# Hybrid decoder step: larger triangular base blocks on VectorE, chains over the prompt ahead in the scheduler's order, samples spaced wider

## The chip, the cores and the metric

The kernel runs on one core of one Trainium2 chip. The metric is the device time of one execution in microseconds (us), of which three were taken. The engines of the core are called PE (TensorE, matrix products), DVE (VectorE), ACT (ScalarE), POOL (GpSimd) and SP (which here issues transfers).

## The reference

One inference step of a trunk of two layers, model width 2048, fp32, for a prompt of 256 tokens and eight samples of one token each, which share the weights. A layer adds to x, in turn, mixers, cross attention and a SwiGLU feed-forward part of width 5632. The mixers are four mLSTM heads and eight heads of gated delta net (GDN) from one input projection. The change concerns the GDN heads. For the prompt, chunk by chunk of 64 tokens:

```python
A = jnp.where(strict, decay_ts * kk * bc[:, None, :, :], 0.0)
rhs = vc - eg[..., None] * jnp.einsum('bthd,bhde->bthe', kc, S)
U = lax.linalg.triangular_solve(A, rhs, left_side=True, lower=True, unit_diagonal=True)
wu = bc[..., None] * U
o = eg[..., None] * einsum(qc, S) + einsum(qk, wu)
S_new = exp(g_end) * S + einsum(wend, kc, wu)
```

For a sample the same recurrence is one step: products of its key and query with the state S (128x128 for each head and sample), and an update of S by one outer product.

## The kernel before

All tokens stand side by side, 264 columns (256 of the prompt, 8 samples), with the model's width over the partitions. Weights come from memory in blocks of 512 KB (`raw`, four buffers). ACT rounds a block to the fast matmul type (`wh`), DVE subtracts for the remainder (`wl`); `wh` and `wl` have three buffers each. `block` does so for each block, with a scheduling priority of its own (`PRIO`). PE then makes three products for each 128x128 piece (`xh` with `wh`, `xl` with `wh`, `xh` with `wl`), 24 matmuls `acc` a block. This stream of `acc` matmuls goes through the whole kernel; the other work of the mixers stands between its matmuls.

What stands where is set in two steps. First the program's text: `stream` calls `pump` after each pair of pieces, and `pump` advances generators (`chains`) whose due time has come. The clock for this counts only PE's matmuls by their size; a generator says by `yield 13000.0` that it wants to go on that many ns of this clock later. Then a list scheduler orders the instructions on each engine; `tc.high_priority(offset)` moves instructions ahead in its choice. The compiled order is fixed: an engine takes its instructions one after another, and an instruction that waits holds up those behind it.

The GDN heads are handled in four groups of two heads. For each group of each layer three generators run: `gdn_decay` (the gates' decays `E`), `gdn_prompt` and `gdn_sample`.

`gdn_prompt` solves the triangular system by the inverse of four 128x128 matrices at once (two heads, two pairs of chunks). `N` is the strictly lower matrix, `NT` its transpose made by PE, `A` a copy of that. `base_blocks` inverts the diagonal blocks of size `BASE` on DVE: it goes over the columns from the last to the first, with `Dt<-u,Dt` (a product, written into the spare part of `Dt`) and `u<-u,Dt` (a subtraction) for each, and a 32x32-block transpose for each three columns. A last transpose and four copies by ACT (`Dm<-u`) put the blocks into `Dm`, and `Dt` is its transpose. Then `gdn_prompt` doubles the blocks: PE multiplies (`pp<-Dm,A`), DVE masks (`Pf<-pp,up`), PE multiplies again (`pd<-Pf,Dt`), DVE subtracts (`Dm<-Dm,pd`) and transposes `Dm` anew. From 8 this takes four doublings to 128; those from 8 and 16 use full 128x64 matmuls and the masks `up8` and `up16`.

`gdn_sample` gathers the samples' columns on POOL (`kv`, `kqf`), lets PE make `dks` (two transposes and 32 small products with `S`), and works on 8 rows on ACT and DVE (`dkn`, `dqn`, `dvn`, `junk` for squares), to the operands `k3` and `r3` (in the rows `k` and `r`) of the update. `rank1` masks `r3` by four samples at a time (`wm`, eight for each head, two buffers of four), PE makes the outer products `dS`, and DVE adds them to `S`, which is written out. The tiles `kv`, `kqf`, `k3` and `r3` are the same for all groups. `mlstm_sample` does likewise for the mLSTM heads.

Of the kernel before, what the change touches and what calls it, by code (L numbers as in the profile page):

```python
# [27 lines left out]
MEM = 256  # L28
EPS = 1e-6
WB, VB, SB, NV = 10, 6, 7, 6  # L30
BASE = 8
PRIO = 1000
Q0, K0, V0, O0 = 0, 512, 1024, 2048
IF0 = 3072
GQ0, GK0, GV0, GZ0 = 3080, 4104, 5128, 6152
# [13 lines left out]
def kernel(ctx: ExitStack, tc: tile.TileContext, io: dict, outs: list):  # L49
# [16 lines left out]
    clock, chains = [0.0], []  # L66
# [11 lines left out]

    def step(c):
        try:  # L80
            c[0] = next(c[1]) + clock[0]
        except StopIteration:
            chains.remove(c)

    def spawn(gen, after=0.0):
        c = [clock[0] + after, gen]
        chains.append(c)
        return c

# [452 lines left out]
    class Mix:  # L542

        def __init__(self, mx):
            self.mx = mx

        def w(self, name, shape=(4, P)):
            return self.mx.tile([P] + list(shape), F32, name=name, tag="w", bufs=WB)
# [72 lines left out]
    def gdn_prompt(l, g, s, G, M, R):  # L621
        h0 = 2 * g
        q, k, v = s
# [52 lines left out]
        for i in range(4):  # L676
            tr(pa[:, i * P:(i + 1) * P], N[:, i])
        copy(A, four(pa))
        yield 13000.0
        b = BASE  # L680
        while b < P:
            def halves(t, which, i=None):
# [104 lines left out]
    def gdn_sample(l, g, s, G, M, R, S, smp):  # L787

        h0 = 2 * g
        kv, k3, r3, kqf = smp[:4]  # L790
        for kind, at in ((1, 0), (0, 32), (2, 64)):
            pool.tensor_copy(out=kv[:, :, at:at + NB], in_=s[kind][:, :, T:C])
            if kind < 2:
                pool.tensor_copy(out=kqf[:, :, at:at + 41 * 7 + 1:41], in_=s[kind][:, :, T:C])
        yield 7500.0
        while not G.ready:
            yield 500.0
        pks = ps("dks")
        for j in range(2):
            tr(pks[:, T + j * P:T + (j + 1) * P], kv[:, j])  # L800
        for j in range(2):
            for b in range(NB):
                mm(pks[:40, j * P:(j + 1) * P], kqf[:, j, b * 40:(b + 1) * 40], S[:, j, b], b == 0, b == NB - 1)
        kn, qn, vN = M.n("dkn"), M.n("dqn"), M.n("dvn")
        for i, (d, f) in enumerate(((kn, 1.0), (qn, 1.0), (vN, 0.5))):
            copy(d, pks[32 * i:32 * i + NB, T:].rearrange("p (h t) -> p h t", h=2), scale=f)
        qk = M.c("dqk", (2, 2))[:NB]
        c = M.c("dc", (2,))[:NB]
        for j in range(2):
            act.activation(M.junk(NB)[:, :P], kn[:, j], AF.Square, accum_out=qk[:, 0, j:j + 1])  # L810
            act.activation(M.junk(NB)[:, :P], qn[:, j], AF.Square, accum_out=qk[:, 1, j:j + 1])
        dve.tensor_scalar(out=qk, in0=qk, scalar1=4.0 * EPS, scalar2=None, op0=ALU.add)
        power(qk, hm)
        tt(qn, qn, kn, ALU.mult)
        dve.tensor_reduce(out=c, in_=qn, axis=AX.X, op=ALU.add)
        rk, rq = qk[:, 0], qk[:, 1]
        egn, beta = G.gn[:, h0:h0 + 2], G.gn[:, 8 + h0:10 + h0]
        a1, er, bk = (M.c(x, (2,))[:NB] for x in ("da1", "der", "dbk"))
        stt(a1, rk, -1.0, egn, ALU.mult, ALU.mult)
        tt(bk, rk, beta, ALU.mult)  # L820
        dve.tensor_scalar(out=rq, in0=rq, scalar1=DK ** -0.5, scalar2=None, op0=ALU.mult)
        tt(er, rq, egn, ALU.mult)
        tt(c, c, rq, ALU.mult)
        tt(c, c, bk, ALU.mult)
        oN = qn
        for j in range(2):
            stt(vN[:, j], pks[:NB, j * P:(j + 1) * P], a1[:, j:j + 1], vN[:, j], ALU.mult, ALU.add)
            dve.tensor_scalar(out=oN[:, j], in0=pks[32:32 + NB, j * P:(j + 1) * P], scalar1=er[:, j:j + 1],
                              scalar2=None, op0=ALU.mult)
            stt(oN[:, j], vN[:, j], c[:, j:j + 1], oN[:, j], ALU.mult, ALU.add)  # L830
        tt(kn, kn, bc(bk, 2, P), ALU.mult)
        three(k3, kn, False)
        three(r3[:, :, :P], vN, True)
        yield 10000.0
        ev = G.gs[:, h0 * NB:(h0 + 2) * NB].rearrange("p (h b) -> p h b", h=2)
        for j in range(2):
            yield from rank1(S[:, j], k3[:, j], r3[:, j], ev[:, j], M.mx, P)
            nc.sync.dma_start(out=s_S[l, :, h0 + j].rearrange("b k v -> k b v"), in_=S[:, j])
        q = M.c("dq", (2,))[:NB]
        for j in range(2):  # L840
            act.activation(M.junk(NB)[:, :P], oN[:, j], AF.Square, accum_out=q[:, j:j + 1])
        dve.tensor_scalar(out=q, in0=q, scalar1=1.0 / DK, scalar2=EPS, op0=ALU.mult, op1=ALU.add)
        power(q, hm)
        tt(oN, oN, bc(q, 2, P), ALU.mult)
        yield 2500.0
        while R.z is None:
            yield 500.0
        pb = ps("db")
        for j in range(2):
            tr(pb[:, j * NB:(j + 1) * NB], oN[:, j], NB)  # L850
        x = M.c("dx", (2, NB))
        tt(x, pb[:, :2 * NB].rearrange("p (h b) -> p h b", h=2), R.z[:, :, T:C], ALU.mult)
        for j in range(2):
            split_gain(R.hh[:, R.at + j, T:C], R.hl[:, R.at + j, T:C], x[:, j], g_gain(l, h0 + j))
# [35 lines left out]
    def mlstm_decay(h, G, M, R):  # L890

        while not G.ready:
            yield 500.0
        pM = ps("pM")
        spread(pM[:, :T], G, GH + h)
        d = M.e("d", (384,))
        for c, (x, w) in enumerate(((0, T), (T, P))):
            dve.tensor_scalar(out=d[:, x:x + w], in0=pM[:, T - w:T], scalar1=G.gT[:, c, RF + h:RF + h + 1],
                              scalar2=0.0, op0=ALU.subtract, op1=ALU.max)
        act.activation(d, d, AF.Exp, scale=-1.0)  # L900
        for x in (0, T):
            pool.affine_select(out=d[:, x:x + P], in_=d[:, x:x + P], pattern=[[1, P]], compare_op=ALU.is_ge,
                               fill=0.0, base=0, channel_multiplier=-1)
        yield 2800.0
        R.d[h % 2] = d
# [60 lines left out]
    def mlstm_sample(l, g, q, k, vs, G, M, R, Cs, smp):  # L966
        h0 = 2 * g
        kv, k3, r3 = smp[:3]
        if len(smp) == 4:
            smp.append(M.mx.tile([P, 2, 384], F32R, name="kqz", tag="kq"))  # L970
            pool.memset(smp[4].bitcast(F32), 0.0)
# [62 lines left out]
        for j in range(2):  # L1034
            yield from rank1(Cs[j], k3[:, j], r3[:, j], av[:, j], M.mx, DV)
            nc.sync.dma_start(out=s_C[l, :, h0 + j].rearrange("b k v -> k b v"), in_=Cs[j])
        while R.z[1] is None:
            yield 500.0
        yield 500.0
# [10 lines left out]
    def mlstm_inputs(l, g, nx, G, M, R, ncol, st, smp):  # L1050
        w_in = io["w_in"][l]
        h0 = 2 * g
        Cs = []
        for j in range(2):
            Ct = st.tile([P, NB, DV], F32, name="Ct", tag="st")
            nc.gpsimd.dma_start(out=Ct, in_=io["state_mlstm_C"][l, :, h0 + j].rearrange("b k v -> k b v"))
            Cs.append(Ct)
        q, k = M.s("q"), M.s("k")
        scaled(stream(w_in, 0, KT, Q0 + 256 * g, nx), nx, q)
        scaled(stream(w_in, 0, KT, K0 + 256 * g, nx), nx, k, DK ** -0.5)  # L1060
        vs = M.c("mvs", (4, NB))
        for j in range(2):
            spawn(mlstm_decay(h0 + j, G, M, R))
        c = []
        for j in range(2):
            v = M.y("y0")
            scaled(stream(w_in, 0, KT, V0 + 256 * (h0 + j), nx), nx, v)
            pool.tensor_copy(out=vs[:, 2 * j:2 * j + 2], in_=v[:, :, T:C])
            c.append(spawn(mlstm_prompt(l, h0 + j, q, k, v, G, M, R, ncol)))
        c.append(spawn(mlstm_sample(l, g, q, k, vs, G, M, R, Cs, smp)))  # L1070
        return c

# [48 lines left out]
    def mixers(l, nx, mx, st, nx2):  # L1121
# [26 lines left out]
        for g in range(4):  # L1148
            if g % 2 == 0:
                hs[g // 2] = hidden(f"gd{g}")  # L1150
            r = Run()
            r.z, r.E, r.at = None, None, 2 * (g % 2)
            r.formed, r.before = False, R[g - 1] if g else None
            r.hh, r.hl = hs[g // 2]
            R.append(r)
            S = st.tile([P, 2, NB, P], F32, name="S", tag="st")
            for j in range(2):
                nc.gpsimd.dma_start(out=S[:, j], in_=io["state_gdn_S"][l, :, 2 * g + j].rearrange("b k v -> k b v"))
            spawn(gdn_decay(g, G, M, r))
            if g == 0:  # L1160
                s = gdn_inputs(l, g, nx, cb, rawc, M, first)
            else:
                s = gdn_inputs(l, g, nx, cb, rawc, M)
            gd.append(spawn(gdn_prompt(l, g, s, G, M, r)))
            gd.append(spawn(gdn_sample(l, g, s, G, M, r, S, smp)))
            if g:
                gdn_z(l, g - 1, nx, M, R[g - 1])
# [392 lines left out]
```

## Time and profile before

| | |
|---|---|
| times of the three executions, us | 2982.76, 2984.68, 2984.39 |
| median, us | 2984.39 |
| profiled execution, us | 2984.69 |
| its span, us | 2983.0 |
| PE busy | 2913.9 us, 98% |
| DVE busy | 2001.1 us, 67% |
| ACT busy | 1487.2 us, 50% |
| POOL busy | 496.5 us, 17% |
| mean granted clock of PE | 0.992 |

A row of a timeline has start, duration, engine, line and operation, output and inputs with their shapes, the count, and in brackets how long the engine was idle ahead of it and what ended that. A row of waits has the instruction, the one that it waited for, the total, the count and the longest. A row of a stretch of time has the busy time of the engines, the granted clock as a share of full speed, and the use of the DMA engines. The first layer's mixers lie at about 45 to 600 us, the second's at about 1496 to 2055 us; most of the rest is feed-forward.

### The profile page before, as it was taken

Reading aid. Unit: us, or ns where it says so; the run is one execution under the profiler, and the core shown is the slowest. Engines: PE = TensorE matmul, PEld = TensorE weight load, DVE = VectorE, ACT = ScalarE, POOL = GpSimd, SP = SyncE. Lnnn points to the kernel's source line nnn. Section 1 sums busy time; section 2 is a strip of 40 time slices with the busy share of each in tenths; the row PEclk is TensorE's granted clock in tenths of the full one; section 3 lists DMA queues with packets and bytes.
Section 4 is the critical chain, followed back from the end, with each engine's and each line's share of the span. In section 5 each row is a group of like instructions: output and inputs, shape, how many; then the busy total and the mean of one; then the engine's idle time right before and its main releaser. Section 6 shows DMA issues by size and latency. Waiting matters only on the chain.

```text
span 2983.0 us, 57751 instructions
## 1 busy us (share of the span) xinstructions
PE 2913.9 (98%) x23219; PEld 2837.1 (95%) x23219; DVE 2001.1 (67%) x3443; ACT 1487.2 (50%) x2505; POOL 496.5 (17%) x662
## 2 busy tenths in 40 slices
PE   8999999999999999999999999999999999999998
PEld 7899999978999999999999999999799999999998
DVE  7888776877555555555688877778765555555555
ACT  6566554566433333333466555556654343434345
POOL 5222100253100000000132221103520000000001
PEclk9999999999999999999999999999999999999999
DMA  7555465666666666666655554756756666666664
GB/s 194 148 162 154 145 197 163 215 212 189 183 180 181 181 180 181 180 182 179 180 156 160 156 159 139 221 153 212 236 173 178 183 179 183 179 182 180 181 181 132
DMA packets 381252, 530.08 MB, mean 178 GB/s; under 512 B 25576, under 2 KB 226224, under 8 KB 380960
## 3 DMA queue, kind: packets, MB, share of 16 engines
q1 hardware_dynamic: 364328, 498.74, 56.9%
q0 software_dynamic: 7424, 25.20, 2.8%
q10 hardware_dynamic: 9232, 2.45, 0.4%
q8 instruction: 182, 2.98, 0.4%
q14 instruction: 86, 0.70, 0.1%
HBM read 502.88 MB, written 23.83 MB: 177 GB/s over the span
## 4 chain that ended last, share of the span: by engine, by line
PE 86%; DVE 7%; ACT 3%; issue 2%; DMA 1%; POOL 1%; SPq 0%; POOLq 0%; ACTq 0%; DVEq 0%
PE acc L73 76%; DVE wl L61 2%; PE kv L73 2%; DVE xl L58 1%; ACT wh L55 1%; PE dks L73 1%; PE pd L73 1%; PE dS L73 1%; PE pp L73 1%; PE sqC L73 0%; PE pS L73 0%; DVE y L58 0%; DVE xT L61 0%; PE accg L73 0%; DVE p L1355 0%
## 5 line engine op out<-in xcount | busy, mean ns | idle before, releaser
L61 DVE TENSOR_TENSOR wl<-raw,wh 128x1024 fp32r<-128x1024 f32 x880 | 1091.1, 1240 | 794.1 <-ACT wh L55 792.2
L55 ACT ACTIVATE wh<-raw 128x1024 fp32r<-128x1024 f32 x880 | 931.0, 1059 | 1208.7 <-PE acc L73 1085.3
L73 PE MATMUL acc<-xh,wh 128*128 128x264 f32 x4736 | 1369.3, 289 | 6.2 <-ACT wh L55 3.9
L73 PE MATMUL acc<-xh,wl 128*128 128x264 f32 x4736 | 1351.7, 285 | 0.6 <-DVE wl L61 0.5
L73 PE MATMUL acc<-xl,wh 128*128 128x264 f32 x4736 | 1351.3, 285 | 1.1 <-DVE xl L58 1.1
L73 PEld LDWEIGHTS acc<-xh,wh 128*128 128x128 f32 x4736 | 898.3, 190 | 11.2 <-issue 4.3
L73 PEld LDWEIGHTS acc<-xl,wh 128*128 128x128 f32 x4736 | 899.3, 190 | 4.3 <-DVE xl L58 1.7
L73 PEld LDWEIGHTS acc<-xh,wl 128*128 128x128 f32 x4736 | 897.5, 190 | 1.8 <-DVE wl L61 1.6
L73 PE MATMUL acc<-ffh,wh 128*128 128x264 f32 x1408 | 400.8, 285 | 0.6 <-DVE xT L61 0.5
L73 PE MATMUL acc<-ffl,wh 128*128 128x264 f32 x1408 | 400.8, 285 | 0.0
L73 PE MATMUL acc<-ffh,wl 128*128 128x264 f32 x1408 | 400.3, 284 | 0.0
L61 POOL TENSOR_TENSOR fg<-fg,rstd 128x264 f32<-128x264 f32 x88 | 94.4, 1102 | 1306.0 <-ACT fg L1442 1286.3
L73 PEld LDWEIGHTS acc<-ffh,wh 128*128 128x128 f32 x1408 | 264.8, 188 | 1.0 <-issue 1.0
L73 PEld LDWEIGHTS acc<-ffl,wh 128*128 128x128 f32 x1408 | 265.3, 188 | 0.0
L73 PEld LDWEIGHTS acc<-ffh,wl 128*128 128x128 f32 x1408 | 265.0, 188 | 0.0
L61 DVE TENSOR_TENSOR xT<-acc,xT 128x264 f32<-128x264 f32 x512 | 190.8, 424 | 19.5 <-PE acc L73 18.9
L61 POOL TENSOR_TENSOR sa<-sa,sq 128x264 f32<-128x264 f32 x96 | 95.4, 1011 | 177.2 <-ACT sq L317 176.9
L55 ACT ACTIVATE wm<-r,msk 72x128 fp32r<-72x128 f32 (+1 forms) x192 | 68.6, 425 | 21.2 <-PE dS L73 16.1
L58 DVE SCALAR_TENSOR_TENSOR xl<-xT,cst,xh 128x264 fp32r<-128x264 f32 x96 | 77.3, 842 | 0.5 <-ACT xh L55 0.5
L58 DVE SCALAR_TENSOR_TENSOR y<-y,cst,y 128x255 f32<-128x255 f32 (+1 forms) x144 | 64.7, 480 | 0.3
L55 ACT ACTIVATE xh<-xT,cst 128x264 fp32r<-128x264 f32 x80 | 39.6, 507 | 29.0 <-DVE xT L61 29.0
L61 POOL TENSOR_TENSOR vl<-vc,vh 128x512 fp32r<-128x512 f32 x32 | 44.4, 1414 | 24.7 <-ACT vh L55 24.7
(516 smaller groups left out, 3332.4 us busy)
## 6 DMA issues: line engine op xcount, KB each, us to landing
raw<-in_w_in_dram SPq DMA_DIRECT2D x224, 512.0 KB
raw<-in_ffn_w_gate_dram SPq DMA_DIRECT2D x176, 512.0 KB
raw<-in_ffn_w_up_dram SPq DMA_DIRECT2D x176, 512.0 KB
raw<-in_ffn_w_down_dram SPq DMA_DIRECT2D x176, 512.0 KB
raw<-in_w_out_dram SPq DMA_DIRECT2D x64, 512.0 KB
S<-in_state_gdn_S_dram POOLq DMA_DIRECT2D x16, 512.0 KB, 6.3
out_dram<-S SPq DMA_DIRECT2D x16, 512.0 KB
Ct<-in_state_mlstm_C_dram POOLq DMA_DIRECT2D x8, 1024.0 KB, 6.8
```

Of the source, the lines that this page charges most:

```text
L55: act.activation(out, in_, AF.Copy, scale=scale)
L58: dve.scalar_tensor_tensor(out=out, in0=a, scalar=s, in1=b, op0=o0, op1=o1)
L61: (eng or dve).tensor_tensor(out=out, in0=a, in1=b, op=op)
L73: pe.matmul(out=out, lhsT=lhsT, rhs=rhs, start=start, stop=stop)
```

## The change

It has four parts. `BASE` is 16: DVE inverts 16x16 blocks (15 columns instead of 7, each column for half as many blocks), and the doubling from 8 with its `pp`, `pd`, mask, subtraction and transpose is gone. The generators `gdn_decay` and `gdn_prompt` run with a scheduling priority of 400, those of the mLSTM's decay and prompt with 200. In `gdn_prompt` 20000 ns instead of 13000 lie between `NT` and the first doubling. The samples' generators wait for each other (`M.sampling` is held from the gathering of the columns to the last state's write-out), and their steps are spaced by 10500 and 12000 ns instead of 7500 and 10000.

```diff
--- before.py
+++ after.py
@@ -28,8 +28,9 @@
 MEM = 256
 EPS = 1e-6
 WB, VB, SB, NV = 10, 6, 7, 6
-BASE = 8
+BASE = 16
 PRIO = 1000
+AHEAD = 400
 Q0, K0, V0, O0 = 0, 512, 1024, 2048
 IF0 = 3072
 GQ0, GK0, GV0, GZ0 = 3080, 4104, 5128, 6152
@@ -78,12 +79,13 @@
 
     def step(c):
         try:
-            c[0] = next(c[1]) + clock[0]
+            with tc.high_priority(offset=c[2]):
+                c[0] = next(c[1]) + clock[0]
         except StopIteration:
             chains.remove(c)
 
-    def spawn(gen, after=0.0):
-        c = [clock[0] + after, gen]
+    def spawn(gen, after=0.0, ahead=0):
+        c = [clock[0] + after, gen, ahead]
         chains.append(c)
         return c
 
@@ -542,7 +544,8 @@
     class Mix:
 
         def __init__(self, mx):
-            self.mx = mx
+
+            self.mx, self.sampling = mx, False
 
         def w(self, name, shape=(4, P)):
             return self.mx.tile([P] + list(shape), F32, name=name, tag="w", bufs=WB)
@@ -676,7 +679,7 @@
         for i in range(4):
             tr(pa[:, i * P:(i + 1) * P], N[:, i])
         copy(A, four(pa))
-        yield 13000.0
+        yield 20000.0
         b = BASE
         while b < P:
             def halves(t, which, i=None):
@@ -788,13 +791,18 @@
 
         h0 = 2 * g
         kv, k3, r3, kqf = smp[:4]
+        while M.sampling:
+            yield 500.0
+        M.sampling = True
         for kind, at in ((1, 0), (0, 32), (2, 64)):
             pool.tensor_copy(out=kv[:, :, at:at + NB], in_=s[kind][:, :, T:C])
             if kind < 2:
                 pool.tensor_copy(out=kqf[:, :, at:at + 41 * 7 + 1:41], in_=s[kind][:, :, T:C])
-        yield 7500.0
-        while not G.ready:
-            yield 500.0
+        if not G.ready:
+            while not G.ready:
+                yield 500.0
+            yield 8000.0
+        yield 10500.0
         pks = ps("dks")
         for j in range(2):
             tr(pks[:, T + j * P:T + (j + 1) * P], kv[:, j])
@@ -831,11 +839,12 @@
         tt(kn, kn, bc(bk, 2, P), ALU.mult)
         three(k3, kn, False)
         three(r3[:, :, :P], vN, True)
-        yield 10000.0
+        yield 12000.0
         ev = G.gs[:, h0 * NB:(h0 + 2) * NB].rearrange("p (h b) -> p h b", h=2)
         for j in range(2):
             yield from rank1(S[:, j], k3[:, j], r3[:, j], ev[:, j], M.mx, P)
             nc.sync.dma_start(out=s_S[l, :, h0 + j].rearrange("b k v -> k b v"), in_=S[:, j])
+        M.sampling = False
         q = M.c("dq", (2,))[:NB]
         for j in range(2):
             act.activation(M.junk(NB)[:, :P], oN[:, j], AF.Square, accum_out=q[:, j:j + 1])
@@ -966,6 +975,9 @@
     def mlstm_sample(l, g, q, k, vs, G, M, R, Cs, smp):
         h0 = 2 * g
         kv, k3, r3 = smp[:3]
+        while M.sampling:
+            yield 500.0
+        M.sampling = True
         if len(smp) == 4:
             smp.append(M.mx.tile([P, 2, 384], F32R, name="kqz", tag="kq"))
             pool.memset(smp[4].bitcast(F32), 0.0)
@@ -1034,6 +1046,7 @@
         for j in range(2):
             yield from rank1(Cs[j], k3[:, j], r3[:, j], av[:, j], M.mx, DV)
             nc.sync.dma_start(out=s_C[l, :, h0 + j].rearrange("b k v -> k b v"), in_=Cs[j])
+        M.sampling = False
         while R.z[1] is None:
             yield 500.0
         yield 500.0
@@ -1060,13 +1073,13 @@
         scaled(stream(w_in, 0, KT, K0 + 256 * g, nx), nx, k, DK ** -0.5)
         vs = M.c("mvs", (4, NB))
         for j in range(2):
-            spawn(mlstm_decay(h0 + j, G, M, R))
+            spawn(mlstm_decay(h0 + j, G, M, R), ahead=AHEAD // 2)
         c = []
         for j in range(2):
             v = M.y("y0")
             scaled(stream(w_in, 0, KT, V0 + 256 * (h0 + j), nx), nx, v)
             pool.tensor_copy(out=vs[:, 2 * j:2 * j + 2], in_=v[:, :, T:C])
-            c.append(spawn(mlstm_prompt(l, h0 + j, q, k, v, G, M, R, ncol)))
+            c.append(spawn(mlstm_prompt(l, h0 + j, q, k, v, G, M, R, ncol), ahead=AHEAD // 2))
         c.append(spawn(mlstm_sample(l, g, q, k, vs, G, M, R, Cs, smp)))
         return c
 
@@ -1156,12 +1169,12 @@
             S = st.tile([P, 2, NB, P], F32, name="S", tag="st")
             for j in range(2):
                 nc.gpsimd.dma_start(out=S[:, j], in_=io["state_gdn_S"][l, :, 2 * g + j].rearrange("b k v -> k b v"))
-            spawn(gdn_decay(g, G, M, r))
+            spawn(gdn_decay(g, G, M, r), ahead=AHEAD)
             if g == 0:
                 s = gdn_inputs(l, g, nx, cb, rawc, M, first)
             else:
                 s = gdn_inputs(l, g, nx, cb, rawc, M)
-            gd.append(spawn(gdn_prompt(l, g, s, G, M, r)))
+            gd.append(spawn(gdn_prompt(l, g, s, G, M, r), ahead=AHEAD))
             gd.append(spawn(gdn_sample(l, g, s, G, M, r, S, smp)))
             if g:
                 gdn_z(l, g - 1, nx, M, R[g - 1])
```

Three places show how the order moves; `acc_...` is a stream's accumulator, the number after it tells projections apart, and `s_...`, `k_...`, `r_...`, `y_...` are tiles with their numbers.

PE, first layer, first group: where the first of the samples' outer products `dS` stands. Before:

```order
L77 MATMUL NT<-ident,N 128x128 x4
L73 MATMUL dS<-wm,k_213 128x512
L73 MATMUL acc_1482<-xh,wh 128x264
L73 MATMUL acc_1482<-xl,wh 128x264
L73 MATMUL acc_1482<-xh,wl 128x264
```

and after:

```order
L74 MATMUL acc_1777<-xh,wl 128x264
L74 MATMUL gb<-g_tq,twos 128x256 x2
L74 MATMUL pp<-Dm,A 128x64 x4
L74 MATMUL dS<-wm,k_209 128x512
L74 MATMUL acc_1776<-xh,wh 128x264
L74 MATMUL acc_1776<-xl,wh 128x264
L74 MATMUL acc_1776<-xh,wl 128x264
```

`dS` stood beside the transpose `NT`; it now stands beside the first `pp`, some 190 matmuls of the stream later.

ACT, first layer, second group: what stands around the copies `Dm<-u` that the first `pp` waits for. Before:

```order
L55 ACTIVATE wh<-raw 128x1024 x2
L858 ACTIVATE s_2603<-y 128x528
L55 ACTIVATE wh<-raw 128x1024
L55 ACTIVATE Dm<-u 32x4x32 x4
L55 ACTIVATE dkn<-dks 8x256
L55 ACTIVATE dqn<-dks 8x256
L55 ACTIVATE dvn<-dks 8x256
L810 ACTIVATE junk,dqk<-dkn 8x128
```

and after:

```order
L819 ACTIVATE junk,dqk<-dqn 8x128
L56 ACTIVATE wh<-raw 128x1024
L818 ACTIVATE junk,dqk<-dkn 8x128
L819 ACTIVATE junk,dqk<-dqn 8x128
L56 ACTIVATE k_209<-dkn 8x256 x2
L56 ACTIVATE r_210<-dvn 8x2x128 x2
L850 ACTIVATE junk,dq<-dqn 8x128 x2
L56 ACTIVATE wm<-r_210,msk 72x128 x8
L56 ACTIVATE Dm<-u 32x4x32 x4
L56 ACTIVATE wh<-raw 128x1024 x2
```

The copies stood ahead of the samples' copies from `dks`; they now stand behind all of that group's work on ACT up to the eight `wm`.

DVE, second layer, second group: from the `wl` that is the last ahead of the first `pp`'s mask `Pf<-pp`. Before:

```order
L61 TENSOR_TENSOR wl<-raw,wh 128x1024
L61 TENSOR_TENSOR Dt<-u,Dt 128x16x2
L58 SCALAR_TENSOR_TENSOR y<-y_20058,cst,y 128x253 x2
L61 TENSOR_TENSOR u<-u,Dt 128x16x2
L611 STREAM_TRANSPOSE Dt<-u 128x128
L61 TENSOR_TENSOR Dt<-u,Dt 128x16
L61 TENSOR_TENSOR u<-u,Dt 128x16
L58 SCALAR_TENSOR_TENSOR s_20074<-s_20074,y 128x528
L616 STREAM_TRANSPOSE u<-u 128x128
L619 STREAM_TRANSPOSE Dt<-Dm 128x512
L61 TENSOR_TENSOR Pf<-pp,up_97 128x256
```

and the first rows after:

```order
L62 TENSOR_TENSOR wl<-raw,wh 128x1024
L62 TENSOR_TENSOR Dt<-u,Dt 128x8x9
L59 SCALAR_TENSOR_TENSOR s_20108<-s_20108,y 128x528
L59 SCALAR_TENSOR_TENSOR sz<-sz,y_20313 128x528
L62 TENSOR_TENSOR u<-u,Dt 128x8x9
L62 TENSOR_TENSOR Dt<-u,Dt 128x8x8
L62 TENSOR_TENSOR u<-u,Dt 128x8x8
L62 TENSOR_TENSOR Dt<-u,Dt 128x8x7
L62 TENSOR_TENSOR u<-u,Dt 128x8x7
L614 STREAM_TRANSPOSE Dt<-u 128x384
L62 TENSOR_TENSOR Dt<-u,Dt 128x8x6
L62 TENSOR_TENSOR u<-u,Dt 128x8x6
```

Between that `wl` and the last transpose of `u` there stood four instructions of the chain in `u` and `Dt` and one transpose; there now stand eighteen and two, of which ten and one follow behind the rows shown.

## The prediction

> **What bounds the kernel now.** I read the page first, then busy time by stretches, then TensorE's (PE's) waits one by one, and last the timeline around those that the change touches. The page's first part, and two stretches of 50 us (start and end, length; then busy time and count of PE, PEld, DVE, ACT, POOL; the granted clock; DMA share and GB/s), one in the first layer's mixers and one in its feed-forward part:
>
> ```profile
> PE 2913.9 (98%) x23219; PEld 2837.1 (95%) x23219; DVE 2001.1 (67%) x3443; ACT 1487.2 (50%) x2505; POOL 496.5 (17%) x662
> ...
> 100.00:150.00 50.00, 44.42 (x337) 42.86 (x336) 39.91 (x109) 29.62 (x74) 10.84 (x18) 0.93 0.54 156
> 1000.00:1050.00 50.00, 50.00 (x414) 50.00 (x413) 29.53 (x42) 20.35 (x23) 4.38 (x4) 1.00 0.61 183
> ```
>
> PE is the bound. In the feed-forward part it issues a matmul each 0.121 us (50/414) without a gap; in the mixers it is busy 44 of 50 us at a mean clock of 0.93. So time is to be had only where PE waits, runs at the lower clock, or has instructions taken from it. A block of weights is 24 matmuls, 2.9 us. PE's waits, largest first as far as they bear on the change:
>
> ```profile
> PE dS L73 <- ACT wm L55: 8.2, 3, 3.7
> ...
> PE dks L77 <- POOL mvn L926: 4.9, 2, 2.5
> ...
> PE pp L73 <- ACT Dm L55: 4.1, 1, 4.1
> ...
> PE dks L77 <- POOL kv L792: 2.1, 2, 1.9
> PE mkT L77 <- DVE vn L61: 2.0, 1, 2.0
> PE mvT L77 <- DVE N L58: 1.8, 1, 1.8
> ...
> PE pS L73 <- DVE wu L61: 0.8, 1, 0.8
> ```
>
> The rows `dS` and `dks` are the samples' products, the rest the chain over the prompt. Together 23.9 us, the most that this change can take away in waits. The longest single one, in order of time on VectorE (DVE), ScalarE (ACT) and PE:
>
> ```profile
> 1667.59 1.21 DVE L61 TENSOR_TENSOR wl<-raw,wh 128x1024 fp32r<-128x1024 f32 x1
> 1668.72 0.18 DVE L61 TENSOR_TENSOR Dt<-u,Dt 128x32 f32<-128x32 f32 x1
> 1668.83 0.87 DVE L58 SCALAR_TENSOR_TENSOR y<-y,cst,y 128x253 f32<-128x253 f32 x2
> ...
> 1670.46 0.71 DVE L58 SCALAR_TENSOR_TENSOR s<-s,y 128x528 f32<-128x528 f32 x1
> 1671.09 0.30 DVE L616 STREAM_TRANSPOSE u<-u 128x128 f32<-128x128 f32 x1
> ...
> 1671.42 1.26 ACT L55 ACTIVATE Dm<-u 32x128 f32<-32x128 f32 x4 [1.00 <-DVE u L616]
> ...
> 1672.83 1.68 PE L73 MATMUL pp<-Dm,A 128*128 128x64 f32 x8 [4.12 <-ACT Dm L55]
> ```
>
> This is how such a wait arises. `wh` and `wl` have three buffers each, so block k can be split only when PE has finished block k-3; what stands behind `wl` in DVE's order cannot start sooner, however idle DVE was before. Here 5.2 us of work stand between `wl` and the first `pp`, and PE gets there first.
>
> **The change part by part.** *Two product steps fewer in each group of GDN heads.* With blocks of 16, one `pp` and one `pd` step go, in four groups of two layers: 16 steps. One step, and a sample's state product:
>
> ```profile
> 129.06 1.00 PE L73 MATMUL pp<-Dm,A 128*128 128x64 f32 x8
> 129.87 0.37 PE L73 MATMUL acc<-xh,wh 128*128 128x264 f32 x1
> ...
> 133.43 0.47 PE L77 MATMUL dks<-ident,kv 128*128 128x128 f32 x2 [1.86 <-POOL kv L792]
> 133.83 5.28 PE L73 MATMUL dks<-S,kqf 128*40 128x128 f32 x32
> ```
>
> The stream goes on 0.81 us after the step began, and the step stood in its way whole: with PE the bound, 16 x 0.83 = 13.3 us less (0.83 with the start of a `pd`, estimated).
>
> *A longer chain on DVE.* In each group 30 instructions, `Dt<-u,Dt` and `u<-u,Dt` by turns, replace 14, and five transposes of 128x384 replace two, and one of 128x128. The rows of the chain, and of what goes with a product step:
>
> ```profile
> 272.32 0.57 DVE L611 STREAM_TRANSPOSE Dt<-u 128x384 f32<-128x384 f32 x1
> 272.92 0.22 DVE L61 TENSOR_TENSOR Dt<-u,Dt 128x64 f32<-128x64 f32 x1
> 273.18 0.22 DVE L61 TENSOR_TENSOR u<-u,Dt 128x64 f32<-128x64 f32 x1
> 273.44 0.21 DVE L61 TENSOR_TENSOR Dt<-u,Dt 128x48 f32<-128x48 f32 x1
> ...
> 140.18 0.42 DVE L61 TENSOR_TENSOR Dm<-Dm,pd 128x256 f32<-128x256 f32 x1 [8.09 <-PE pd L73]
> 140.64 0.71 DVE L714 STREAM_TRANSPOSE Dt<-Dm 128x512 f32<-128x512 f32 x1
> ...
> 144.05 0.42 DVE L61 TENSOR_TENSOR Pf<-pp,up 128x256 f32<-128x256 f32 x1
> 144.47 0.43 DVE L61 TENSOR_TENSOR y<-acc,rstd 128x264 f32<-128x264 f32 x1
> ```
>
> The former start 0.25 us apart. Chain before: 14 x 0.25 + 2 x 0.57 + 0.30 = 4.9 us; after: 30 x 0.25 + 5 x 0.57 = 10.4 us, 5.5 more. What goes with the steps (a mask 0.42, a subtraction 0.41, a transpose 0.71) takes 1.5 off DVE's total. DVE had 10 us free in the 50 shown, so its added 4 us a group cost nothing as load; they cost where PE waits for their end.
>
> *Samples later, and one after another.* In PE's order the first layer's `dks` moves from 396 to 540 stream matmuls, its `dS` from 492 to 678, and likewise for the next groups. The `dks` on POOL's `kv` and `mvn` and the `dS` on `wm` come far behind their inputs, and those waits go; also those of `mvT`, `mkT`, `pS` and the old `pp`, whose neighbours moved. I take off all 23.9. SP and POOL issue the same transfers, moved with the samples. On POOL the load of the next state stands behind the write-out of the one before the last, and the powers, the convolution's sums and the copy of the unit matrix into `u` stand behind that load:
>
> ```profile
> S<-in_state_gdn_S_dram POOLq DMA_DIRECT2D x16, 512.0 KB, 6.3
> ```
>
> The load itself takes 6.3 us to land and is used a group later; if the write-out holds POOL as long (estimated alike, the same 512 KB), that is two blocks, and what stands behind is used three or more later in the order. I cost it at nothing; without that cover it would be up to 6.3 us at each of six loads, part of the upper bound below.
>
> *What is late next: the first `pp` of a group.* It stands 48 to 66 stream matmuls later than before, but its chain is 5.5 us longer, and in ACT's order the samples' `wm` now stand ahead of `Dm`. The prices on ACT, from the place after the `dks` above:
>
> ```profile
> 145.67 0.63 ACT L858 ACTIVATE sz<-y 128x528 f32<-128x528 f32 x1
> ...
> 150.53 0.42 DVE L61 TENSOR_TENSOR r<-dvn,r 8x256 fp32r<-8x256 f32 x1
> ...
> 150.33 0.31 ACT L841 ACTIVATE junk<-dqn 8x128 f32<-8x128 f32 x1
> ...
> 152.04 1.85 ACT L55 ACTIVATE wm<-r,msk 72x128 fp32r<-72x128 f32 x6
> 153.80 1.04 ACT L55 ACTIVATE wh<-raw 128x1024 fp32r<-128x1024 f32 x1
> ```
>
> Eight `wm` 2.4 us, a `junk` with its read-out 0.4, `sz` 0.6, `wh` 1.0, `Dm` 1.26. I go through the eight first `pp` as in the place at 1667.59: from the moment that the ring frees a buffer, the work that stands in order up to the end of `Dm`, less the time PE needs from there to the `pp`.
> First layer. Group 0: `wh` 1.0 + `junk` 0.4 + eight `wm` 2.4 + `sz` 0.6 + `Dm` 1.3 = 5.7, PE there after 1.1: waits 4.6. Group 1: the sample's `dks` stands 24 matmuls ahead. Before, `r` ended 17.5 us after `dks` began (133.43 to 150.95); of these some 3.5 are weight splits and projections that no longer stand between, 1.6 more are instructions of the chain that now do; then `wm` 2.4 and `Dm` 1.3: 19.3, PE there after 5.6 + 2.9 = 8.5: 10.8. Group 2: eight `wm` hold `wh` back by 1.5; `wh` 1.0, `wl` 1.1, five of the chain 1.25, transpose 0.3, `Dm` 1.3 = 6.4 less 0.8: 5.6. Group 3: the same without the 1.5, 4.9 less 0.7: 4.2.
> Second layer. Group 0: two `wh` 2.0, two `junk` 0.8, eight `wm` 2.4, two projections 0.9, `Dm` 1.3 = 7.4 less 3.9: 3.5. Group 1: a projection 0.4, `wl` 1.1, eighteen of the chain 4.5, two transposes 1.1 and one 0.3, two gate products (as `s` at 1670.46) 1.4, `Dm` 1.3 = 10.1, and PE stands there from the start: 10.1. Group 2: `wh` 1.0, `wl` 1.1, transpose 0.6, six of the chain 1.5, eleven small operations of the sample (0.24 each, an estimate between the chain's rows and `r`) 2.6, transpose 0.3, `Dm` 1.3 = 8.4 less 2.4: 6.0. Group 3: none.
> Sum 44.8 us, against 4.1 before. The same reckoning gives shorter new waits at a `dS` on `qT`'s squares (2.1), the mLSTM's `mC` (1.6), a `kk` (2.2) and smaller places: 8 us. Bounds: nothing, if each input comes just in time, as at seven of eight such places before; and 70, if every one of these is late by 2 us more, as far as the ring's moment is missed when a wait throws DVE and ACT out of step. I take 52.8, since the one place that the trace shows reads the same way.
>
> *The clock after a wait.* A `dks` after a wait of 2.4 us, and rows of the clock (PE's busy time and count, then the granted clock): two behind the `dS` wait of 3.7 us, one behind the `dks` at 272.36, one behind that at 133.43.
>
> ```profile
> 272.36 0.44 PE L77 MATMUL dks<-ident,kv 128*128 128x128 f32 x2 [2.36 <-POOL mvn L926]
> ...
> 110.00:111.00 1.00, 1.00 (x5) 0.50 0.78 182
> 113.00:114.00 1.00, 1.00 (x10) 0.89 0.06 16
> ...
> 278.00:279.00 1.00, 1.00 (x9) 1.00 0.00 0
> ...
> 134.00:135.00 1.00, 1.00 (x6) 0.50 1.14 388
> ```
>
> After most waits of 1.8 us or more PE runs at half clock for some 3.4 us (also at 134, after only 1.86), which costs about 1.5 us; after the one at 272.36 it did not. Six such dips behind removable waits, one twice as long: 10 us less. Of eleven new waits I count eight with a dip: 12 us more.
> The Trainium skill (TensorE: Matmul & The Clock Gate, "Part 1: The HAM clock gate") says that the clock falls to half after a whole idle window of about 3.4 us and returns after 3.4 us of work. The return agrees with the rows; the fall does not, since 1.86 us did it at 134. By the page only waits over 3.4 us would throttle, two before (3 us) and seven after (10.5 us), and the sum below would be 5.5 us higher.
>
> **The sum.** -13.3 (steps) - 23.9 (old waits) - 10 (old dips) + 52.8 (new waits) + 12 (new dips) = +17.6. The profiled execution took 2984.69 us (span 2983.0 and 1.7 around it), 0.3 above the median of 2984.39, so 3002 us, 0.6% slower. What measurement can tell from no change is 0.2%, 6 us.
>
> **The rivals.** *The first `pp` is in time.* Steps, waits and dips go, little comes: 2984.4 - 47 = 2937 at best, 2970 where half the new waits come (26 + 6). Seven of the eight first `pp` before had no wait, which speaks for it; the longer chain behind the same ring speaks against. It decides below 73% of my new waits: 0.73 x 64.8 = 47. Chance 0.24, most of it between 2955 and 2978.
> *It cancels.* Four fifths of the new waits, or old waits that stay at `mvT` and `mkT`: within 6 us of before. Chance 0.13.
> *DVE falls behind for longer.* When PE waits for `Dm`, `wl` behind it is late too, and DVE with 40 of 50 us busy needs several blocks to get its lead back, so the next `pd` and `pp` wait as well. At 2 us for each of seven places, 14 more: 3016. Chance 0.13. My forecast itself: 0.50, from 2992 to 3012.
> Range: from the middle of the first rival, 2960, to 3022. Faster by over 0.2% 0.24, within it 0.13, slower 0.63.
>
> **What would show it.** In the changed profile: `pd` and `pp` 16 steps fewer, DVE's total up by some 30 us; the waits of PE headed by `pp` on `Dm`, seven of them and over 40 us in all, the longest two near 10 us in the second group of each layer; `dS` on `wm` and `dks` on POOL gone from the list; clock 0.5 for 3 us behind each. The feed-forward stretches unchanged. I am wrong if `pp` waits less than 30 us in all: then ACT's order does not hold `Dm` as I read it, and the time is below 2984.

## The result and the profile after

The changed kernel took 3008.6 us (3006.43 to 3011.83, four runs) against 2984.53 us for the kernel before on the same chip: a ratio of 1.0079, 95% interval 1.0066 to 1.0093, so 24 us slower. The forecast was 3002. The first part of the page after:

```profile
PE 2906.2 (97%) x23091; PEld 2828.9 (94%) x23091; DVE 2020.5 (67%) x3562; ACT 1486.8 (49%) x2505; POOL 500.2 (17%) x660
```

PE is busy 8 us less and issues 128 records less, the sixteen steps. The span is 22.9 us longer (3005.9 against 2983.0), so PE stands still 30.6 us more than before (99.7 against 69.1). PE's waits after (instruction, what it waited for, total, count, longest), those of the mixers:

```profile
PE pp L74 <- ACT Dm L56: 31.0, 5, 10.2
PE pp L74 <- issue: 10.2, 1, 10.2
...
PE pp L74 <- POOL y L62: 3.7, 1, 3.7
...
PE dS L74 <- ACT junk L673: 2.1, 1, 2.1
PE kk L74 <- ACT eL L594: 2.1, 1, 2.1
PE mC L74 <- DVE kw L62: 1.7, 1, 1.7
PE sqC L74 <- DVE sl L62: 1.6, 1, 1.6
...
PE kk L74 <- DVE dqn L836: 1.0, 1, 1.0
...
PE pp L74 <- ACT Co L56: 0.8, 1, 0.8
```

`dS` on `wm`, `dks`, `mkT` and all but 0.5 us at `mvT` are gone; `pp` has taken their place. Where the row says "issue" or POOL's `y`, the count and the place show that it is a first `pp` too: the profile names the event that it saw last. One by one, in PE's timeline:

```profile
134.28 1.94 PE L74 MATMUL pp<-Dm,A 128*128 128x64 f32 x8 [4.75 <-ACT Dm L56]
227.97 1.97 PE L74 MATMUL pp<-Dm,A 128*128 128x64 f32 x8 [10.20 <-ACT Dm L56]
308.15 1.92 PE L74 MATMUL pp<-Dm,A 128*128 128x64 f32 x8 [5.01 <-ACT Dm L56]
392.20 1.97 PE L74 MATMUL pp<-Dm,A 128*128 128x64 f32 x8 [4.66 <-ACT Dm L56]
...
1610.89 1.07 PE L74 MATMUL pp<-Dm,A 128*128 128x64 f32 x8 [3.65 <-POOL y L62]
1698.60 1.94 PE L74 MATMUL pp<-Dm,A 128*128 128x64 f32 x8 [10.19 <-issue]
1782.87 1.97 PE L74 MATMUL pp<-Dm,A 128*128 128x64 f32 x8 [6.37 <-ACT Dm L56]
1858.29 1.10 PE L74 MATMUL pp<-Dm,A 128*128 128x64 f32 x8 [0.84 <-ACT Co L56]
```

Place by place the forecast was 4.6, 10.8, 5.6, 4.2, 3.5, 10.1, 6.0 and none: 44.8 us against 45.7. What ends such a wait, at the first of them, on DVE and ACT:

```profile
130.91 1.22 DVE L62 TENSOR_TENSOR wl<-raw,wh 128x1024 fp32r<-128x1024 f32 x1
132.04 0.15 DVE L851 TENSOR_SCALAR dq<-dq 8x2 f32<-8x2 f32 x1
132.11 0.15 DVE L62 TENSOR_TENSOR Dt<-u,Dt 128x8 f32<-128x8 f32 x1
132.30 0.19 DVE L62 TENSOR_TENSOR u<-u,Dt 128x8 f32<-128x8 f32 x1
132.52 0.31 DVE L619 STREAM_TRANSPOSE u<-u 128x128 f32<-128x128 f32 x1
...
129.79 2.43 ACT L56 ACTIVATE wm<-r,msk 72x128 fp32r<-72x128 f32 x8
132.13 0.62 ACT L867 ACTIVATE sz<-y 128x528 f32<-128x528 f32 x1
132.87 1.26 ACT L56 ACTIVATE Dm<-u 32x128 f32<-32x128 f32 x4
```

ACT comes to `Dm` at 132.75, behind the eight `wm` and `sz`, as forecast. But DVE's last transpose of `u` ends at 132.83: both engines arrive together, and taking either away alone would bring little. At the other places one of them comes last. At 308.15, 392.20 and 1698.60 it is DVE: ACT had been idle for 2.6, 3.1 and 6.8 us and begins the copies within 0.04 us of the transpose's end. At 227.97, 1610.89 and 1782.87 it is ACT, which begins them 1.84, 1.57 and 0.63 us after that end. The first of these three:

```profile
224.53 0.31 DVE L619 STREAM_TRANSPOSE u<-u 128x128 f32<-128x128 f32 x1
...
226.68 1.25 ACT L56 ACTIVATE Dm<-u 32x128 f32<-32x128 f32 x4
```

How full DVE is ahead of the seven first `pp` that wait (start and end, length, then busy time and count of PE, PEld, DVE, ACT, POOL, the clock, the DMA share and GB/s):

```profile
118.00:129.50 11.50, 11.50 (x95) 11.32 (x93) 11.30 (x31) 7.35 (x13) 2.39 (x2) 1.00 0.57 169
208.00:218.00 10.00, 9.78 (x81) 9.21 (x80) 7.75 (x25) 4.76 (x14) 1.74 (x2) 1.00 0.81 250
290.00:303.00 13.00, 13.00 (x108) 12.92 (x106) 12.47 (x40) 9.65 (x26) 3.02 (x4) 1.00 0.61 173
360.00:370.00 10.00, 10.00 (x79) 9.76 (x79) 9.21 (x27) 5.41 (x10) 3.02 (x5) 1.00 0.44 142
1590.00:1607.00 17.00, 17.00 (x141) 17.00 (x139) 16.64 (x47) 12.34 (x32) 3.77 (x9) 1.00 0.48 143
1675.00:1688.00 13.00, 13.00 (x108) 13.00 (x107) 12.25 (x27) 5.70 (x7) 7.20 (x8) 1.00 0.92 270
1760.00:1776.00 16.00, 16.00 (x135) 15.48 (x134) 13.52 (x39) 8.83 (x22) 1.52 (x4) 1.00 0.51 145
```

DVE works 92 to 98% of five of these stretches, and 78 and 85% of the other two, of which the first stands ahead of the longest wait. The mean over the kernel, 67%, says nothing of that. But a full DVE alone makes no wait: in the kernel before it is busy for 10.62 of the 11 us from 118 to 129, and the first `pp` at 129.06 does not wait.

### The profile page after: what moved, and what is told of

It reads as the page before. It is cut to its first block, busy times and chain, and to the rows that moved or that the text cites. A ratio compares the mean times of both kernels' runs of the same rounds, so it can differ in the third digit from the quotient of the medians.

```text
span 3005.9 us, 57606 instructions
## 1 busy us (share of the span) xinstructions
PE 2906.2 (97%) x23091; PEld 2828.9 (94%) x23091; DVE 2020.5 (67%) x3562; ACT 1486.8 (49%) x2505; POOL 500.2 (17%) x660
## 5 line engine op out<-in xcount | busy, mean ns | idle before, releaser
L62 DVE TENSOR_TENSOR wl<-raw,wh 128x1024 fp32r<-128x1024 f32 x880 | 1090.6, 1240 | 788.3 <-ACT wh L56 787.0
L56 ACT ACTIVATE wm<-r,msk 72x128 fp32r<-72x128 f32 (+1 forms) x192 | 68.7, 425 | 17.3 <-PE dS L74 16.7
L74 PE MATMUL pp<-Dm,A 32*32 32x32 f32 (+2 forms) x256 | 22.8, 250 | 45.8 <-ACT Dm L56 31.0
L74 PEld LDWEIGHTS pp<-Dm,A 32*32 32x32 f32 (+2 forms) x256 | 19.5, 160 | 49.9 <-ACT Dm L56 27.1
L59 DVE SCALAR_TENSOR_TENSOR y<-y,cst,y 128x255 f32<-128x255 f32 (+2 forms) x144 | 64.2, 475 | 0.9 <-ACT y L56 0.4
```

The costliest lines, as they stand in the source:

```text
L56: act.activation(out, in_, AF.Copy, scale=scale)
L59: dve.scalar_tensor_tensor(out=out, in0=a, scalar=s, in1=b, op0=o0, op1=o1)
L62: (eng or dve).tensor_tensor(out=out, in0=a, in1=b, op=op)
L74: pe.matmul(out=out, lhsT=lhsT, rhs=rhs, start=start, stop=stop)
```

## The experiments

Four theories were set against each other. A: the first `pp` waits for what stands in order, on DVE and ACT, between a freed weight buffer and `Dm`. B: the samples' `wm` ahead of `Dm` on ACT make the waits. C: the chain on DVE alone is too long. E, formed after the first four runs: DVE is full ahead of each first `pp`, so its load decides. Rivals of single runs stand in their expectations. Times are medians; "before" is the kernel before on the same chip beside them (2985.61 us for the first four runs below, 2986.21 for the priority and the three with silu on POOL, 2984.14 for the others).

**The copies on POOL.**

```diff
-            copy(Dm[r:r + 32, :, r:r + 32], N3[r:r + 32])
+            pool.tensor_copy(out=Dm[r:r + 32, :, r:r + 32], in_=N3[r:r + 32])
```

> The changed kernel with the four copies Dm<-u of each group on POOL instead of ACT; DVE's and PE's orders stay as they are. Theory A (the first pp waits for all that stands, in DVE's and ACT's order, between a freed weight buffer and Dm; both engines share in it): the parts due to ACT's wm and wh go, those due to the chain on DVE stay: first layer 3.0, 7.5, 5.0, 4.7, second 0, 10.2, 6.2, sum 37 instead of 46, time 2996 to 3001. Theory B (the samples' wm ahead of Dm on ACT make the waits): sum below 15, time 2965 to 2975. Theory C (the chain on DVE alone is too long): no change, 3008.

3009.83 us, 24.2 over before: no change. PE's waits there:

```profile
PE pp L74 <- POOL Dm L621: 44.8, 7, 10.2
```

44.8 us at the same seven places. Theory B falls. A's figure falls as well: ACT's share was to be 9 us. Where ACT had come last, the wait is 1.2 us shorter in the first layer's second group (9.0) and 0.4 in the second layer's third (6.0), and 1.1 longer in the second layer's first (4.7), where POOL takes 3.69 us for what took ACT 1.25. In the first group the copies start on POOL 0.1 us behind the end of `u`'s transpose and take 1.82 us. So where ACT came last, DVE's chain stood only 0.6 to 1.8 us behind it, 4 us in all, and POOL's slower copies take back most of that. Theory C had forecast the time; the runs without taps below speak against it.

**The gap ahead of the first doubling, shorter and longer.**

```diff
-        yield 20000.0
+        yield 13000.0     # the first run; 22000.0 in the second
```

> The changed kernel with the 13000 ns of before between NT and the first doubling instead of 20000; all else as changed. Theory A: more of the chain stands behind the last wl when PE reaches the first pp (9 to 23 instructions of the chain in five groups instead of 2 to 18), waits at the first pp 60 to 75 us instead of 46, time 3022 to 3035. Rival D (the later pp costs as much as it saves, since what follows it comes later too): waits at pp rise but others fall, time within 6 us of 3008.

> The changed kernel with 22000 ns instead of 20000. Theory A: in most groups two instructions of the chain are left behind the last wl, seven in the second group of the second layer; waits at the first pp about 29 us instead of 46, time 2987 to 2994. Rival D: time within 6 us of 3008. If only ACT's order counted (theory B), the waits would stay near 46.

With 13000: 3040.28 us, 54.7 over before. The first `pp` waits 73.6 us (60.7 + 7.8 + 5.1 by its three rows), as theory A has it; the time is 5 us over its range. Rival D falls here.

With 22000: 3007.71 us, 22.1 over before, the same as the changed kernel within the intervals (1.0059 to 1.0089). The waits at the first `pp` fall to 30.0 us, as forecast, and the time does not follow. Its rows:

```profile
PE pp L74 <- ACT Dm L56: 27.7, 5, 10.1
PE mvT L78 <- DVE kw L62: 3.0, 1, 3.0
...
PE pp L74 <- issue: 2.3, 1, 2.3
...
PE mkT L78 <- DVE N L59: 1.5, 1, 1.5
```

PE stands still only 6.4 us less than in the changed kernel (93.3 against 99.7), though the first `pp` waits 15.7 less. In the second layer 4.5 us are back at `mvT` and `mkT`, whose inputs DVE makes, with one half-clock stretch more; from its gates' first product with `gl` to the `ssq` behind its mixers it takes 587.9 us instead of 582.0, while the first layer takes 10.2 less from `pg` on. Ahead of `pg` 3.3 us are lost in the profiled execution, at half clock from about 40 to 47 us, which has nothing to do with the gap: the runs with 13000 and with the copies on POOL show the same stretch. Without it this execution would be some 2 us shorter than the changed kernel's, still far from A's 2987 to 2994. Rival D was right for the time: past a point the wait is not removed by a later `pp` but turns up behind other products.

**The samples' part alone.** The changed kernel with `BASE = 8`, `AHEAD = 0` and the 13000 ns of before.

> Of the change only the samples' part: one sample's generator at a time and the wider spacing; BASE 8, 13000 ns, no priority. Theory A: dS and dks go from the list of PE's waits (15 us and their dips), the old waits at mvT and mkT and one or two at the first pp stay (8 to 14 us): 2968 to 2980. Theory B (the later samples put wm ahead of Dm): new waits at the first pp of 20 us or more, 2990 to 3000.

2990.27 us, 4.7 over before (ratio 1.0009 to 1.0028); neither theory's range. `dS` on `wm` and `dks` are gone, but 11.6 us stand at two first `pp` of the second layer and 2.8 at `NT`. In DVE's order seven instructions of the chain and six taps stand behind the last `wl` ahead of the longer of the two (7.7 us). The old waits were exchanged, not removed. That the samples' part is a loss is not shown, though: in the profiled execution the first layer takes 6.9 us less and the second 6.9 more, from the gates' first product to `ssq`, and the 3.9 us by which its span is longer arise ahead of both: the first product of the gates comes at 41.9 us instead of 37.8.

**BASE 16 alone.**

```diff
-BASE = 8
+BASE = 16     # in the kernel before
```

> The kernel before with BASE 16 and nothing else: the samples and the 13000 ns as before. Theories A and E: 16 steps go (13 us), but four to twenty-two instructions of the chain stand behind the last wl at all eight first pp, which wait 45 to 55 us in all, and the old dS and dks waits stay (10 to 15 us): 3020 to 3032. Rival (BASE 16 alone is a gain, the other parts spoil it): below 2980.

3039.77 us, 55.6 over before, and 8 us over the range. The rows:

```profile
PE pp L73 <- ACT Dm L55: 43.4, 6, 11.1
PE dS L73 <- ACT wm L55: 10.8, 4, 3.9
PE pp L73 <- issue: 9.9, 1, 9.9
```

53.3 us at seven first `pp`, as forecast (for eight). The rival, that BASE 16 alone is a gain, falls. Of the four parts of the change this one carries the loss. Beside the changed kernel with 13000 ns, which has all the rest but the gap and lies as far above before (54.7), it shows that the longer gap gives back 31 us (3040.28 to 3008.6) and that the samples' part and the priority together give back nothing that can be measured while the gap is 13000.

**The priority.**

```diff
-AHEAD = 400
+AHEAD = 0
```

> The changed kernel with priority 0 for the chains over the prompt. PE's order is the same row for row, DVE's differs in places. If the priority does what its words say (chains first), its removal makes the waits at the first pp longer, 50 to 60 us, time 3012 to 3025. Theory E (DVE full ahead of each first pp, so its order decides little): within 6 us of 3008, waits 44 to 48.

3008.25 us: the same as with it. The first `pp` waits 44.9 us. The words "chains over the prompt first" do not describe what happens: DVE's order differs in some places, and the time stays.

**The chain cut short, the steps still saved.**

```diff
-        for k0 in range(BASE - 1, 0, -3):
+        for k0 in range(7, 0, -3):
```

> The changed kernel with the columns 8 to 15 of the 16x16 blocks left out on DVE (16 of the 30 instructions of a group's chain and two transposes less, 5 us); all else, the saved product steps too, as changed. Theory A and theory E (DVE is full ahead of each first pp, so that PE waits for what DVE has too much): each first pp waits 5 us less, 46 becomes about 10, five dips go: 2960 to 2972. Rival G (the wait is due to the place of pp and to the samples' work, not to the chain): waits over 30 us, time over 2990.

2952.7 us, 31.4 under before (ratio 0.9883 to 0.9913) and 56 under the changed kernel; 7 us below the range; rival G falls. This kernel leaves out a part of the inversion, so it serves to measure and not as a version to use. All that is left at a first `pp`:

```profile
PE pp L74 <- issue: 3.8, 1, 3.8
```

This is the cleanest of the runs: the change without the added 16 instructions and two transposes a group is a clear gain, and with them a loss. They are 5 us a group by the forecast's prices, 4.5 by DVE's busy time (2020.5 less 1984.8), and they cost 7 us a group on PE. Nor does it depend on how full DVE is: here too DVE is all but full ahead of the first group's `pp`, but the chain has ended by 114.1 us, and the `pp` at 132.1 does not wait.

```profile
118.00:129.50 11.50, 11.50 (x96) 11.50 (x95) 11.37 (x29) 8.14 (x18) 3.92 (x5) 1.00 0.50 139
```

**DVE relieved elsewhere.** The three shifted taps of the convolution left out, in the changed kernel and in the one before; neither kernel computes the whole then.

```diff
-                for d in (1, 2, 3):
+                for d in ():
```

> The changed kernel with the three shifted taps of the convolution left out (18 scalar_tensor_tensor of 0.45 us a group, 8 us of DVE, none of them in the chain); the chain and its place stay. Theory E (DVE's load): waits at the first pp fall from 46 to 5 to 15, time 2955 to 2970. Theory A in its narrow form (the chain's own length behind a freed buffer, with 0.25 us for each of its instructions): waits stay over 35, time over 2998.

> The kernel before with the same taps left out, a control for the run without taps of the changed kernel. Theory E: the 4 us at its one pp go, and mvT, mkT perhaps; dS and dks on the samples' chain stay: 2965 to 2978, so that the changed kernel without taps is as fast as this one or faster. Theory A in its narrow form: the changed kernel without taps stays 20 us slower than this one.

Changed without taps: 2973.75 us, 35 less than with them. Before without taps: 2954.33 us, 30 less and 11 below its range: `dks` no longer waits and `dS` on `wm` only 2.2 us, though they were to stay. The first `pp` of the changed kernel:

```profile
PE pp L74 <- ACT Dm L56: 10.4, 3, 4.6
PE pp L74 <- issue: 7.6, 1, 7.6
```

With the 0.8 of a third row 18.8 us, between the two theories' figures and nearer to E; the time lies between them too. The taps are 8 us a group by the expectation's price, 6.3 by DVE's busy time (2020.5 less 1970.0). This work is no part of the chain and is worth 30 to 35 us, some 4 us a group, in either kernel: the load counts, and theory C falls, since the chain is as long as before. But 19.4 us remain between the two kernels, nearly all of the difference with taps (24): what the longer chain costs, a lighter DVE does not cure. Theory A in its narrow form had said that, and its figure for the waits was wrong. The first layer's last group still waits 4.6 us (4.66 with taps): no taps lie ahead of it.

**A version that might be faster.** The second half of silu of q, v and z from DVE to POOL, as a product and a sum, in three kernels: before, after, and the samples' part alone. The second half for k stays on DVE.

```diff
         act.activation(out, y, AF.Tanh, scale=0.5)
-        stt(out, out, 1.0, y, ALU.add, ALU.mult)
+        tt(out, out, y, ALU.mult, pool)
+        tt(out, out, y, ALU.add, pool)
```

> The kernel before with the second half of silu of q, v and z in the GDN groups on POOL (a product and a sum) instead of one 0.7 us instruction on DVE; 2.1 us of DVE a group less, some 11 us of POOL more. Theory E, with the 30 us that 8 us a group were worth without the taps: 8 us less, 2974 to 2979. Rival H (POOL's slower silu, and the shared way to memory, delay what follows): 2984 or more, new waits at qT or vT or dks.

> The changed kernel with silu of q, v and z on POOL as in the run beside it. Theory E: a quarter of what the taps were worth (35 us): 2998 to 3002, waits at the first pp 36 to 41 us. Narrow theory A: 3006 to 3010. Rival H: above 3010.

> The samples' part of the change alone (BASE 8, 13000 ns, no priority), with silu of q, v and z on POOL. Theory E: the 11.6 us at the second layer's first pp and the 2.9 at NT fall, 8 to 12 us less than the 2990 of the samples' part alone: 2978 to 2982. Rival H: 2990 or more.

3003.26 us (17.1 over before), 3017.31 (31.1 over) and 3010.62 (24.4 over): rival H in all three. DVE's busy time rose, from 2001.1 to 2013.4 us in the first, although 16.7 us were taken from it. The last section shows where. In the changed kernel the first `pp` did wait less, 38.6 us, within E's 36 to 41; `dks` on POOL's `kv` came back with 5.5. No run with the full computation beat the kernel before.

## Why the prediction was right, point by point

**The sum.** By the same terms, forecast and measured (profiled executions; the half clock is half the time at 0.5 behind each wait, without the wait itself):

| term | forecast, us | measured, us |
|---|---|---|
| product steps | -13.3 | not measured alone |
| old waits | -23.9 | -23.4 |
| old half-clock stretches | -10 | -13.2 |
| waits at the first `pp` | +44.8 | +45.7 |
| other new waits | +8 | +8.5 |
| new half-clock stretches | +12 | +19.7 |

With -13.3 for the steps the measured terms give +24.0, the span grew by 22.9; 0.9 of the difference is a shorter half-clock stretch at the kernel's end (3.8 us lost against 4.7). So the steps' worth is confirmed to about 1 us, by difference only. The forecast was 6.4 us short of this sum: 4.5 in the clock, the rest spread over the waits.

**What failed: the clock term.** It was mis-sized: +6.5 net instead of +2. The stretch at half clock was taken as 3.4 us for every wait. After the change it lasts up to 6.9 us; two rows behind the wait that ended at 308.15 (busy time and count of PE, then the clock):

```profile
312.00:313.00 1.00, 1.00 (x6) 0.50 0.00 0
314.00:315.00 1.00, 1.00 (x7) 0.50 0.00 0
```

The count was nearly right: seven new waits have such a stretch, eight were forecast. And one reading was plainly wrong: the prediction said that the `dks` wait at 272.36 had no such stretch, from a row at 278. It had one, from 273.65 to 277.06:

```profile
274.00:275.00 1.00, 1.00 (x7) 0.50 0.98 339
276.00:277.00 1.00, 1.00 (x6) 0.50 0.00 0
```

The clock has to be read right behind the wait, not five us later. Read in steps of 0.1 us, the two traces show more. After the change the clock stands at half from 134.16 to 140.99, 222.91 to 233.15, 308.24 to 315.07, 390.16 to 396.99, 1612.13 to 1615.54, 1690.64 to 1704.29 and 1779.39 to 1789.63: two, three, two, two, one, four and three times 3.41 us, partly within the wait. All the ends lie whole multiples of 3.413 us apart (233.15 less 140.99 is 27 of them, 1615.54 less 315.07 is 381). So in one execution the clock changes only on a fixed grid of 3.413 us, and a wait falls on it wherever it happens to. What counts is PE's idle time within one stretch of the grid. Between 60 and 2900 us, where such a stretch ran at full clock, twenty in the two traces held 1.86 us or more of idle time, and half clock followed each; none with 1.83 or less was followed by it:

| stretch | PE idle in it, us | clock in the next |
|---|---|---|
| before, 130.29 to 133.70 | 1.86 | 0.50 |
| before, 331.68 to 335.09 | 1.83 | 1.00 |
| after, 615.44 to 618.85 | 1.76 | 1.00 |
| after, 2165.09 to 2168.51 | 1.96 | 0.50 |

In the traces of nine of the experiments the limit is a little less sharp: 1.61 us were enough once, 1.88 not enough twice. So a wait of 2.48 us after the change (ended at 619.57) cost no clock, since the grid divided it, and the one of 1.86 at 133.43 did. Where the waits fall on the grid differs between executions: with the priority at 0 the first `pp` wait as long (44.9 us), and the half clock costs 46.3 us over the profiled execution instead of 37.9. The 19.7 above is one draw.

The Trainium skill (TensorE: Matmul & The Clock Gate, "Part 1: The HAM clock gate") says that the window of 3.4 us runs freely and that at least one busy window is needed. The grid agrees with the first. Why behind some waits one such stretch is enough and behind others two are needed is open: the waits that end at 109.70 before and at 308.15 after end 0.11 and 0.09 us ahead of the grid, and 3.41 us at half clock follow the one, 6.83 the other. The other half of the Trainium skill's rule, that a whole idle window comes first, does not hold here, as 1.86 us of 3.41 were enough. By that rule the prediction counted two stretches before and seven after; there were seven among the old waits and seven among the new.

**What was right for half the reason: the new waits.** Their sizes came from counting what stands behind a freed buffer, and that held at each of eight places and again at 22000 ns. But the prediction said of DVE that "its added 4 us a group cost nothing as load", from the mean of a 50 us stretch. DVE is 78 to 98% busy ahead of the first `pp` that wait, and load there costs PE time (the two runs without taps). Why the count comes out so well is argued, not shown: a DVE that is nearly full works through its order almost without a pause, so that the order gives the time. It had the last engine right at the five places where one came last by more than 1 us. Theory A's split of the waits between ACT and DVE was wrong: where ACT came last, DVE was close behind, so that taking the copies off ACT brought 0.9 us and not 9. The count also fails away from this kernel: without taps it gave over 35 us, and 18.8 were measured. Its forecast of some 30 us more on DVE was too large as well: 19.4 (2020.5 less 2001.1), since the smallest instructions of the chain, as the `Dt<-u,Dt` of 128x8 above, are busy 0.15 to 0.19 us and not the 0.25 that lie between two starts.

**The old waits** went as forecast. That they go was no gain in itself: the samples' part alone is not faster than before.

**The rivals.** That the first `pp` is in time, at 2937 to 2970, needed the chain to fit ahead of it; with the chain cut short it is at all but one place (3.8 us), and the time is 2952.7. That DVE falls behind for longer did not show: only the first `pp` of each group waits, no `pd` for over 0.2 us.

## What to carry to other kernels

Where one engine sets the end and a second feeds it in a fixed order, the second one's mean load tells nothing of the places where it is needed. Look at the 10 to 20 us ahead of each product that needs it, and count what stands in the order between the last freed buffer and that product's input. How full the engine is does not foretell a wait by itself: twice here it was 97 and 99% busy and nothing waited. The count foretold each of the eight waits to within a microsecond in this kernel, and failed once other work was taken away. Work added to the chain cost the first engine more than itself, 7 us for 4.5 to 5; work beside the chain cost it less, some 4 us for 6 to 8. When waits are shifted by spacing steps wider, add up all waits of the stretch and the clock behind them: a wait that leaves one instruction and returns at the next has moved, not gone.

## What the runs showed that was not expected

POOL holds DVE up. In the kernel before with silu on POOL, while POOL works on a product of two tiles, some of DVE's small instructions with two inputs take up to nine times as long. DVE and POOL in the timeline:

```profile
290.08 1.27 DVE L61 TENSOR_TENSOR dkn<-dkn,dbk 8x256 f32<-8x256 f32 x1
291.28 1.27 DVE L61 TENSOR_TENSOR der<-dqk,gn 8x2 f32<-8x2 f32 x1
...
288.97 3.57 POOL L61 TENSOR_TENSOR sz<-sz,y 128x528 f32<-128x528 f32 x2 [0.54 <-ACT sz L858]
```

`der` is 8x2 elements and takes 1.27 us here; over its eight places, before and with silu on POOL (count, busy time, mean ns, idle time ahead), it is so slow at three:

```profile
L61 DVE TENSOR_TENSOR der<-dqk,gn 8x2 f32<-8x2 f32 x8 | 1.1, 142 | 0.0
...
L61 DVE TENSOR_TENSOR der<-dqk,gn 8x2 f32<-8x2 f32 x8 | 4.5, 566 | 0.0
```

Here it ends with POOL's second instruction, at 292.55. `wl`, of two inputs and 1.24 us, hardly shows it (1244 ns against 1240 over 880). The Trainium skill (GPSIMD Engine Reference, "8. Key points") says that the two share their way to memory, with contention for DVE's instructions of two inputs or in a two-port mode; the trace agrees for two inputs, and gives the price, up to 1.1 us for an instruction of 0.14. Some rows of one input rose as well (`qd` of 128x4 from 201 to 362 ns); whether these ran in such a mode is not shown here. The rows of `dkn` and `der` together rose by 6.9 us, of the 29 that the rest of DVE rose; the others are spread over many rows.
